# A hybrid mLSTM/RWKV-7 layer: PSUM banks, chain steps over two pairs, and the place of preparation and chain in the order

## Chip, cores and metric

The kernel runs on one core of a Trainium2 chip. The metric is the device time of one execution in microseconds. The median of three runs before the change is 3376.81 us (3371.88 to 3381.96).

## What is computed

One layer of a diffusion backbone over 512 latent tokens of width 2048, with 256 context tokens as a prefix, all in float32.

1. The condition vectors (one for the latents, one for the context) go through silu and the matrix w_mod and give shifts, scales and gates (the "modulation", 12288 columns).
2. The RMS-normalised and modulated tokens go through one input projection w_in. Half of the heads are mLSTM (4 heads), the others RWKV-7 (16 heads of 64, handled in 8 pairs of 128 channels), each in both directions. Context runs first; the latent scans start from the context's final states.
3. RWKV-7 per token: `S = S diag(w) - (S kk)(kk*a)^T + v k^T`, `y = S r`. Both directions are added, normalised per head, a bonus term is added, and the sum is multiplied with a gate.
4. Both halves are concatenated, go through w_out, and are added to x with a gate. A gated feed-forward part follows (up and gate projection, 3x3 depthwise convolution on the 8x64 grid, GELU, down projection), then a last RMS norm.

## The kernel before, in words

**Matmuls.** A weight tile is loaded (`wload`, L337), split into a high part and a rest (`whi` on ACT, `wlo` on DVE, L299 and L300), and each product is made of three matmuls (L370 to L372 for tiles of 128 channels by 512 tokens, L403 to L405 for token-major ones). The projection of one 128-column tile for the latents is 48 matmuls.

**RWKV in chunks of 64 tokens.** It has three stages per pair of heads. *Preparation* (`pair_shared`, `prep`, `bonus`): decays, keys and removal vectors are computed on ACT and DVE, then per half of the 512 columns two PSUM tiles take key-by-key products (L747), DVE masks them into `r_Gp` (L750), PE transposes the decayed keys (L759), ACT copies them into `r_sg` (L763), and everything goes to DRAM as the chunks' operands (`Sc_d` for the context, `Sx_d` for the latents). A context pair does both directions at once; a latent pair does one after the other. `bonus` (L931) ends a latent pair's preparation with the ACT copy of L941. The SBUF tiles of preparation (`r_kr`, `r_sg`, `r_KR`, `r_BK`, `r_Gp`, ...) have one buffer each. *Solve* (`tsolve`): the triangular systems of all chunks of two pairs are inverted, first 32x32 blocks by 30 steps on DVE (L798, L799), then two rounds of small matmuls (L816, L821). *Chain* (`chain`, `chain_step`): the state goes from chunk to chunk, 4 chunks for the context, 8 for the latents, both directions in one call: products with the state and with V, an ACT copy (`r_Rs`, L872), products, an ACT copy (`r_U`, L880), products, then DVE updates the states (L892) and adds the outputs (L899, L901). A call takes one pair, and has two PSUM banks; the two pairs of a job take turns, c by c.

**PSUM.** All eight banks are given to three tags (L126): `acc` for projections, `pre` for preparation, modulation sums, normalisation sums and the mLSTM heads, `R` for solve and chain (and L209).

**Order.** The program is traced in one order; a list scheduler then gives each instruction to its engine's queue by a simulated timeline: among those that could start, the one with the lowest number goes first. `tc.high_priority(n)` takes n off the numbers inside it. In the kernel before, only weight loads and splits have that, with 3000 (L343). Each engine runs its own queue strictly in the order that comes out. In the traced order, the loop over latent pairs (L1222) does: projections of the next pair, then `x_job(p)` (L1154): for even p from 2 a solve of two pairs, for odd p from 3 a chain of two pairs, then preparation of pair p; after it mLSTM gates (for p = 0) and a piece of the late modulation (`ada_late`, DVE sums over w_mod, L232). Behind the loop come the last solve, the last chain, the four mLSTM heads' projections (`x_head`), and the mLSTM heads themselves (`mlstm_head`; those marked early use preparation's SBUF tiles, the solve's `t_X` among them). The output projection is in two halves; the first (`out_first`, L1267) needs mLSTM heads 0 and 1 and RWKV pairs 0 to 3.

Of the kernel before, what the change touches and what calls it, by code (L numbers as in the profile page):

```python
# [11 lines left out]
ALU = mybir.AluOpType  # L12
# [3 lines left out]
P = 128  # L16
# [70 lines left out]
FIN_O = 1  # L87
EARLY_AT = (1, 2, 4, 4)
PRELOAD = True
TCOPT = dict(schedule_with_timeline_sim=True)  # L90


# [4 lines left out]
def body(tc, A, dbg=None):  # L97
# [25 lines left out]
    wp = Pool("wp")  # L123
    hp = Pool("hp")
    sm = Pool("sm")
    PB = {"acc": 2, "pre": 2, "R": 4}  # L126

    def PS(tag, shape):
        return ps.tile(list(shape), F32, tag=tag, name=nm(tag), bufs=PB[tag])
# [14 lines left out]
    rk = Pool("rk")  # L144
# [504 lines left out]
    LOHI = (slice(0, 64), slice(64, 128))  # L649
# [9 lines left out]
    def pair_shared(p, seg):  # L659
        n = NX if seg == "x" else NC_  # L660
        s = K()
        s.kr = rp("r_kr", [P, NX])
        s.kk = rp("r_kk", [P, NX])
        sp.dma_start(s.kr[:, :n], kr_d[seg][p])
        act.activation(s.kk[:, :n], s.kr[:, :n], AF.Copy, scale=V("rkk", p))
        sq = rp("r_t1", [P, NX])
        act.activation(sq[:, :n], s.kk[:, :n], AF.Square)
        pn = PS("pre", [P, 512])
        pe.matmul(pn[:, :n], bones, sq[:, :n], start=True, stop=True)
        act.activation(sq[:, :n], pn[:, :n], AF.Ln, bias=BK12)  # L670
        act.activation(sq[:, :n], sq[:, :n], AF.Exp, scale=-0.5)
        dve.tensor_tensor(s.kk[:, :n], s.kk[:, :n], sq[:, :n], ALU.mult)
        if seg == "x":
            s.r = rp("r_r", [P, NX])
            sp.dma_start(s.r, r_d[p])
        s.up = rp("r_up", [P, 2, 2, P])
        sp.dma_start(s.up, A["rup"][p])
        return s
# [159 lines left out]
            sp.dma_start(t[hs], v_d[seg][p // 2, :, :, o:o + 64].rearrange("a (b t) v -> t (a b) v", t=64))  # L838
        return t

    def chain_step(us, ops, cs, V, y, first, last):

        x = us[0].seg == "x"
        kc = us[0].kc
        bank = [PS("R", [P, 8, 64]) for _ in range(2)]
        pos = (0, 1) if cs[0] < cs[1] else (1, 0)
        opened = {}

        def mm(h, half, o, w, rhs):

            hs = LOHI[h]
            out = bank[h][LOHI[half], o, :]
            at = opened.get((h, half))
            f = dict(stop=True, skip_group_check=True)
            if at is None:
                opened[(h, half)] = pe.matmul(out, w[hs], rhs[hs], start=True, **f)
                return
            with tc.issue_after(at.ins):
                pe.matmul(out, w[hs], rhs[hs], start=False, **f)  # L859

        w = [o[:, c % 2] for o, c in zip(ops, cs)]
        kinds = range(2) if x else range(1)
        for src in range(2):
            for k, u in enumerate(us):
                for j in kinds:
                    for h in range(2):
                        o = 2 * kc * src + 64 * j
                        mm(h, h if j == 0 else 1 - h, pos[k], w[k][:, o:o + 64], u.M if src == 0 else V[:, cs[k], :])
        Rs = rk("r_Rs", [P, 2, 64], 3)
        U = rk("r_U", [P, 2, 64], 3)  # L870
        for h, hs in enumerate(LOHI):
            act.copy(Rs[hs], bank[h][hs, 0:2, :])  # L872
        for k, u in enumerate(us):
            for h in range(2):
                mm(h, 1 - h, 2 + pos[k], w[k][:, kc:kc + 64], Rs[:, pos[k], :])
            for h in range(2):
                if not last:
                    mm(h, h, 2 + pos[k], w[k][:, 3 * kc + 64:3 * kc + 128], V[:, cs[k], :])
        for h, hs in enumerate(LOHI):
            act.copy(U[hs], bank[h][LOHI[1 - h], 2:4, :])  # L880
        for k, u in enumerate(us):
            for h in range(2):
                if not last:
                    mm(h, h, 2 + pos[k], w[k][:, 3 * kc:3 * kc + 64], U[:, pos[k], :])
            for h in range(2):
                if x:
                    mm(h, 1 - h, pos[k], w[k][:, kc + 64:kc + 128], U[:, pos[k], :])
        if not last:
            for k, u in enumerate(us):
                g = u.g0 + cs[k]  # L890
                for h, hs in enumerate(LOHI):
                    dve.scalar_tensor_tensor(u.M[hs], u.M[hs], u.gC[hs, g:g + 1], bank[h][hs, 2 + pos[k], :], ALU.mult, ALU.add)  # L892
        if x:
            lo, hi = min(cs), max(cs)
            for h in range(2):
                hs = LOHI[1 - h]
                out = y[hs, lo:hi + 1:hi - lo, :]
                if first:
                    dve.tensor_copy(out, bank[h][hs, 0:2, :])  # L899
                else:  # L900
                    dve.tensor_tensor(out, bank[h][hs, 0:2, :], out, ALU.add)  # L901

    def chain(pairs, mid):

        x = pairs[0][0].seg == "x"
        nch = pairs[0][0].nch
        Vs, ys = [], []
        for us in pairs:
            Vs.append(chain_v(us[0].p, us[0].seg, nch))
            ys.append(rk("r_yt", [P, 8, 64], 2) if x else None)  # L910
            for u in us:
                if not x:
                    Mst[(u.p, u.d)] = rk("r_M", [P, 64], 16)
                    pool.memset(Mst[(u.p, u.d)], 0.0)
                u.M = Mst[(u.p, u.d)]
        n = nch // 2
        for i in range(n):
            if x and i == 1:
                mid()
            ops = [[chain_load(u, i if u.d == 0 else n - 1 - i) for u in us] for us in pairs]  # L920
            for c in range(2 * i, 2 * i + 2):
                for us, o, V, y in zip(pairs, ops, Vs, ys):
                    chain_step(us, o, (c, nch - 1 - c), V, y, c < nch // 2, x and c == nch - 1)
        if x:
            for us, y in zip(pairs, ys):
                y_d = us[0].y_d = DT("yr_d", [4, P, 128], 8)
                for h in range(2):
                    sp.dma_start(y_d[:, :, 64 * h:64 * h + 64].rearrange("a (b t) v -> t (a b) v", t=64), y[LOHI[1 - h]])
            mid()
# [215 lines left out]
    def ctx_job(p):  # L1145
        do_chain()
        job = []
        for pp in range(p, p + 2):
            s = pair_shared(pp, "c")
            job.append((pp, prep(pp, s, "c", DT("Sc_d", [P, 8, 320], 8)), None))  # L1150
        do_solve()
        solve_q.append(job)

    def x_job(p):  # L1154
        if p < 2:
            do_chain()
        elif p % 2 == 0:
            do_solve(2)
        else:
            do_chain(2)  # L1160
        s = pair_shared(p, "x")
        S_d = DT("Sx_d", [P, 16, 512], 8)
        us = prep(p, s, "x", S_d, 0) + prep(p, s, "x", S_d, 1)
        job = [(p, us, bonus(p, us[0], us[1], s))]
        if p == 0:
            do_solve()
        solve_q.append(job)
# [333 lines left out]
```

## Time and profile before

| | |
|---|---|
| median of 3 runs | 3376.81 us |
| profiled execution | 3379.97 us, span 3378.2 us |
| mean granted clock of TensorE | 0.945 |
| PE, PE weight loads, DVE, ACT busy | 3108.0, 2509.7, 2165.9, 1192.4 us |
| DMA | 548.53 MB, 162 GB/s on average |

The span runs from the first to the last instruction of the profiled execution; the execution's own time is 1.8 us longer. PE is TensorE's matmuls, PEld its weight loads, DVE, ACT and POOL the other engines, SP the queue that issues most DMAs. A granted clock of 1.0 is TensorE's full rate. "Releaser" is what ended a wait by the semaphores' records.

### The profile page before, as it was taken

The numbers are of one execution on the slowest core, as the hardware profiler recorded it, in microseconds if no ns is written. First come the engines' busy times: TensorE is split into PE (matmuls) and PEld (weight loads), VectorE is DVE, ScalarE is ACT, GpSimd is POOL, SyncE is SP. The second block draws the span as 40 slices with busy tenths as digits, with TensorE's granted clock in tenths as the row PEclk, the third lists the DMA queues.
The fourth block names the chain that finished last, engine by engine and source line by source line (L and its number), as shares of the span: only waits on it lengthen the run. The fifth ranks groups of instructions, "written<-read, shape, count | busy, mean of one in ns | idle before, by whom it ended". The sixth has DMA issues, their size and how long they took to land.

```text
span 3378.2 us, 54574 instructions
## 1 busy us (share of the span) xinstructions
PE 3108.0 (92%) x21030; PEld 2509.7 (74%) x21030; DVE 2165.9 (64%) x4178; ACT 1192.4 (35%) x2414; POOL 59.6 (2%) x113
## 2 busy tenths in 40 slices
PE   8998899999989898657599899999999999999998
PEld 5687777777768687545477688888888888888887
DVE  2587776688688778645644788455555555555657
ACT  4355554344444344222223432222222222322323
POOL 0000100010000000000000000000000000000000
PEclk9999998899989898767799999999999999999999
DMA  8877555557767687565844255222223222222232
GB/s 284 305 243 220 155 159 163 166 174 234 208 208 239 215 247 240 181 197 178 257 153 157 77 199 194 94 94 98 95 95 99 94 96 98 94 98 96 94 100 100
DMA packets 394387, 548.53 MB, mean 162 GB/s; under 512 B 151664, under 2 KB 272776, under 8 KB 393872
## 3 DMA queue, kind: packets, MB, share of 16 engines
q1 hardware_dynamic: 384480, 531.67, 49.3%
q10 hardware_dynamic: 9648, 13.37, 1.1%
q8 instruction: 166, 2.72, 0.3%
q14 instruction: 93, 0.76, 0.1%
HBM read 457.49 MB, written 87.47 MB: 161 GB/s over the span
## 4 chain that ended last, share of the span: by engine, by line
PE 53%; DMA 9%; DVE 6%; ACT 1%; issue 1%; SPq 1%; DVEq 0%; ACTq 0%
PE acc L371 10%; PE acc L372 10%; PE acc L370 10%; PE acc L1376 5%; PE acc L1378 5%; PE acc L1377 5%; DMA am<-in_wmod 3%; PE acc L1262 1%; PE pre L621 1%; PE acc L1263 1%; PE acc L1264 1%; DVE adacc L232 1%; DMA Sx_d<-r_sg 1%; PE R L859 1%; DMA x_d<-ev 1%
## 5 line engine op out<-in xcount | busy, mean ns | idle before, releaser
L299 ACT CAST whi<-wraw 128x512 fp32r<-128x512 f32 (+1 forms) x948 | 569.6, 604 | 1307.7 <-PE acc L371 678.6
L300 DVE TENSOR_TENSOR wlo<-wraw,whi 128x512 fp32r<-128x512 f32 (+1 forms) x948 | 628.4, 666 | 429.0 <-ACT whi L299 423.1
L370 PE MATMUL acc<-H,whi 128*128 128x512 f32 x1920 | 761.2, 396 | 6.1 <-ACT ev L520 4.0
L372 PE MATMUL acc<-H,wlo 128*128 128x512 f32 x1920 | 762.3, 397 | 1.2 <-DVE wlo L300 1.2
L371 PE MATMUL acc<-H,whi 128*128 128x512 f32 x1920 | 760.4, 396 | 0.0
L370 PEld LDWEIGHTS acc<-H,whi 128*128 128x128 f32 x1920 | 363.8, 189 | 87.5 <-ACT ev L520 4.3
L372 PEld LDWEIGHTS acc<-H,wlo 128*128 128x128 f32 x1920 | 364.2, 190 | 82.0 <-issue 4.9
L371 PEld LDWEIGHTS acc<-H,whi 128*128 128x128 f32 x1920 | 364.4, 190 | 78.8 <-issue 2.9
L1380 DVE SCALAR_TENSOR_TENSOR x<-acc,mod,x 128x512 f32<-128x512 f32 (+1 forms) x192 | 135.6, 706 | 221.7 <-PE acc L1378 221.6
L1324 DVE SCALAR_TENSOR_TENSOR f_cv<-upad,fvec,f_cv 128x512 f32<-128x512 f32 x352 | 263.8, 749 | 7.2
L1376 PE MATMUL acc<-fh,whi 128*128 128x512 f32 x640 | 253.2, 396 | 0.0
L1377 PE MATMUL acc<-fl,whi 128*128 128x512 f32 x640 | 253.1, 396 | 0.0
L1378 PE MATMUL acc<-fh,wlo 128*128 128x512 f32 x640 | 253.1, 396 | 0.0
L232 DVE SCALAR_TENSOR_TENSOR adacc<-am,csil,adacc 128x512 f32<-128x512 f32 x240 | 179.4, 748 | 83.7 <-DMA am<-in_wmod 81.6
L403 PE MATMUL acc<-whi,H 128*128 128x256 f32 x512 | 159.8, 313 | 2.2 <-ACT r_E L720 1.5
L405 PE MATMUL acc<-wlo,H 128*128 128x256 f32 x512 | 158.6, 311 | 1.6 <-DVE wlo L300 1.6
L404 PE MATMUL acc<-whi,H 128*128 128x256 f32 x512 | 156.0, 305 | 0.0
L1378 PEld LDWEIGHTS acc<-fh,wlo 128*128 128x128 f32 x640 | 120.2, 188 | 29.1
L1377 PEld LDWEIGHTS acc<-fl,whi 128*128 128x128 f32 x640 | 120.2, 188 | 29.0
L1376 PEld LDWEIGHTS acc<-fh,whi 128*128 128x128 f32 x640 | 120.2, 188 | 29.0
L1262 PE MATMUL acc<-H,whi 128*128 128x512 f32 x256 | 104.6, 414 | 32.4 <-DVE ev L1271 18.6
L750 DVE TENSOR_TENSOR r_Gp<-pre,c_gmask 64x512 f32<-64x512 f32 (+1 forms) x192 | 115.1, 599 | 18.1 <-DMA Sx_d<-r_Gp 11.6
(346 smaller groups left out, 4751.6 us busy)
## 6 DMA issues: line engine op xcount, KB each, us to landing
am<-in_wmod SPq DMA_DIRECT2D x128, 512.0 KB
wraw<-in_wup SPq DMA_DIRECT2D x88, 512.0 KB
wraw<-in_wgate SPq DMA_DIRECT2D x88, 512.0 KB
wraw<-in_wdn SPq DMA_DIRECT2D x88, 512.0 KB
wraw<-in_wcm SPq DMA_DIRECT2D x72, 512.0 KB
r_GK<-Sx_d SPq DMA_DIRECT2D x64, 512.0 KB
wraw<-in_wtm SPq DMA_DIRECT2D x56, 512.0 KB
Sx_d<-r_Gp SPq DMA_DIRECT2D x32, 512.0 KB
```

The lines of the kernel that those rows point to most:

```text
L232: dve.scalar_tensor_tensor(acc, wm[:, k % 2], csil[:, k:k + 1], acc, ALU.mult, ALU.add)
L299: act.copy(hi, t)
L300: dve.tensor_tensor(lo, t, hi.bitcast(F32), ALU.subtract)
L370: pe.matmul(pt[:, :n], hi(k8), H.h(k), start=k == 0, stop=False)
L371: pe.matmul(pt[:, :n], hi(k8), H.l(k), start=False, stop=False)
L372: pe.matmul(pt[:, :n], lo(k8), H.h(k), start=False, stop=k == KT - 1)
L403: pe.matmul(o, H.h(k)[:, xs], hi(k4), start=first, stop=False, skip_group_check=True)
L405: pe.matmul(o, H.h(k)[:, xs], lo(k4), start=False, stop=k == KT - 1, skip_group_check=True)
L1324: dve.scalar_tensor_tensor(cv, u[:, a:a + GH, b:b + GW], fvec[:, f, tap:tap + 1], cv, ALU.mult, ALU.add)
L1376: pe.matmul(pt, hi(m)[:, k, :], th[:, cs], start=k == 0, stop=False)
L1377: pe.matmul(pt, hi(m)[:, k, :], tl[:, cs], start=False, stop=False)
L1378: pe.matmul(pt, lo(m)[:, k, :], th[:, cs], start=False, stop=k == GF - 1)
```

## The change

`pre` gets four PSUM banks and `R` two. `chain_step` takes the units of all pairs of a job in one call (for a job of two pairs four units), with one pair of banks, one set of `r_Rs` and `r_U` tiles (one buffer each), and copies that are twice as wide; products with V come before those with the state. Chain steps, and the preparation of every pair (`pair_shared`, `prep`, `bonus`), are traced under `high_priority(1500)`. Chunk loads (`chain_load`) and solves are not.

```diff
--- before.py
+++ after.py
@@ -87,6 +87,7 @@
 FIN_O = 1
 EARLY_AT = (1, 2, 4, 4)
 PRELOAD = True
+AHEAD_C = 1500
 TCOPT = dict(schedule_with_timeline_sim=True)
 
 
@@ -123,7 +124,7 @@
     wp = Pool("wp")
     hp = Pool("hp")
     sm = Pool("sm")
-    PB = {"acc": 2, "pre": 2, "R": 4}
+    PB = {"acc": 2, "pre": 4, "R": 2}
 
     def PS(tag, shape):
         return ps.tile(list(shape), F32, tag=tag, name=nm(tag), bufs=PB[tag])
@@ -838,12 +839,12 @@
             sp.dma_start(t[hs], v_d[seg][p // 2, :, :, o:o + 64].rearrange("a (b t) v -> t (a b) v", t=64))
         return t
 
-    def chain_step(us, ops, cs, V, y, first, last):
-
-        x = us[0].seg == "x"
-        kc = us[0].kc
+    def chain_step(units, first, last):
+
+
+        x = units[0][0].seg == "x"
+        kc = units[0][0].kc
         bank = [PS("R", [P, 8, 64]) for _ in range(2)]
-        pos = (0, 1) if cs[0] < cs[1] else (1, 0)
         opened = {}
 
         def mm(h, half, o, w, rhs):
@@ -858,47 +859,48 @@
             with tc.issue_after(at.ins):
                 pe.matmul(out, w[hs], rhs[hs], start=False, **f)
 
-        w = [o[:, c % 2] for o, c in zip(ops, cs)]
-        kinds = range(2) if x else range(1)
-        for src in range(2):
-            for k, u in enumerate(us):
-                for j in kinds:
+        for src in (1, 0):
+            for u, w, c, V, n in units:
+                for j in range(2 if x else 1):
                     for h in range(2):
                         o = 2 * kc * src + 64 * j
-                        mm(h, h if j == 0 else 1 - h, pos[k], w[k][:, o:o + 64], u.M if src == 0 else V[:, cs[k], :])
-        Rs = rk("r_Rs", [P, 2, 64], 3)
-        U = rk("r_U", [P, 2, 64], 3)
+                        mm(h, h if j == 0 else 1 - h, n, w[:, o:o + 64], V[:, c, :] if src else u.M)
+        Rs = rk("r_Rs", [P, 4, 64], 1)
+        U = rk("r_U", [P, 4, 64], 1)
         for h, hs in enumerate(LOHI):
-            act.copy(Rs[hs], bank[h][hs, 0:2, :])
-        for k, u in enumerate(us):
+            act.copy(Rs[hs], bank[h][hs, 0:4, :])
+        for u, w, c, V, n in units:
             for h in range(2):
-                mm(h, 1 - h, 2 + pos[k], w[k][:, kc:kc + 64], Rs[:, pos[k], :])
+                mm(h, 1 - h, 4 + n, w[:, kc:kc + 64], Rs[:, n, :])
             for h in range(2):
                 if not last:
-                    mm(h, h, 2 + pos[k], w[k][:, 3 * kc + 64:3 * kc + 128], V[:, cs[k], :])
+                    mm(h, h, 4 + n, w[:, 3 * kc + 64:3 * kc + 128], V[:, c, :])
         for h, hs in enumerate(LOHI):
-            act.copy(U[hs], bank[h][LOHI[1 - h], 2:4, :])
-        for k, u in enumerate(us):
+            act.copy(U[hs], bank[h][LOHI[1 - h], 4:8, :])
+        for u, w, c, V, n in units:
             for h in range(2):
                 if not last:
-                    mm(h, h, 2 + pos[k], w[k][:, 3 * kc:3 * kc + 64], U[:, pos[k], :])
+                    mm(h, h, 4 + n, w[:, 3 * kc:3 * kc + 64], U[:, n, :])
             for h in range(2):
                 if x:
-                    mm(h, 1 - h, pos[k], w[k][:, kc + 64:kc + 128], U[:, pos[k], :])
+                    mm(h, 1 - h, n, w[:, kc + 64:kc + 128], U[:, n, :])
         if not last:
-            for k, u in enumerate(us):
-                g = u.g0 + cs[k]
+            for u, w, c, V, n in units:
+                g = u.g0 + c
                 for h, hs in enumerate(LOHI):
-                    dve.scalar_tensor_tensor(u.M[hs], u.M[hs], u.gC[hs, g:g + 1], bank[h][hs, 2 + pos[k], :], ALU.mult, ALU.add)
+                    dve.scalar_tensor_tensor(u.M[hs], u.M[hs], u.gC[hs, g:g + 1], bank[h][hs, 4 + n, :], ALU.mult, ALU.add)
         if x:
-            lo, hi = min(cs), max(cs)
-            for h in range(2):
-                hs = LOHI[1 - h]
-                out = y[hs, lo:hi + 1:hi - lo, :]
-                if first:
-                    dve.tensor_copy(out, bank[h][hs, 0:2, :])
-                else:
-                    dve.tensor_tensor(out, bank[h][hs, 0:2, :], out, ALU.add)
+            for k in range(0, len(units), 2):
+                cs = [units[k][2], units[k + 1][2]]
+                lo, hi = min(cs), max(cs)
+                y = units[k][0].y
+                for h in range(2):
+                    hs = LOHI[1 - h]
+                    out = y[hs, lo:hi + 1:hi - lo, :]
+                    if first:
+                        dve.tensor_copy(out, bank[h][hs, k:k + 2, :])
+                    else:
+                        dve.tensor_tensor(out, bank[h][hs, k:k + 2, :], out, ALU.add)
 
     def chain(pairs, mid):
 
@@ -919,8 +921,14 @@
                 mid()
             ops = [[chain_load(u, i if u.d == 0 else n - 1 - i) for u in us] for us in pairs]
             for c in range(2 * i, 2 * i + 2):
-                for us, o, V, y in zip(pairs, ops, Vs, ys):
-                    chain_step(us, o, (c, nch - 1 - c), V, y, c < nch // 2, x and c == nch - 1)
+                units = []
+                for k, (us, os_, V, y) in enumerate(zip(pairs, ops, Vs, ys)):
+                    us[0].y = y
+                    for j, (u, o) in enumerate(zip(us, os_)):
+                        cu = nch - 1 - c if j else c
+                        units.append((u, o[:, cu % 2], cu, V, 2 * k + (j if 2 * c < nch - 1 else 1 - j)))
+                with tc.high_priority(AHEAD_C):
+                    chain_step(units, c < nch // 2, x and c == nch - 1)
         if x:
             for us, y in zip(pairs, ys):
                 y_d = us[0].y_d = DT("yr_d", [4, P, 128], 8)
@@ -1146,8 +1154,9 @@
         do_chain()
         job = []
         for pp in range(p, p + 2):
-            s = pair_shared(pp, "c")
-            job.append((pp, prep(pp, s, "c", DT("Sc_d", [P, 8, 320], 8)), None))
+            with tc.high_priority(AHEAD_C):
+                s = pair_shared(pp, "c")
+                job.append((pp, prep(pp, s, "c", DT("Sc_d", [P, 8, 320], 8)), None))
         do_solve()
         solve_q.append(job)
 
@@ -1158,10 +1167,11 @@
             do_solve(2)
         else:
             do_chain(2)
-        s = pair_shared(p, "x")
-        S_d = DT("Sx_d", [P, 16, 512], 8)
-        us = prep(p, s, "x", S_d, 0) + prep(p, s, "x", S_d, 1)
-        job = [(p, us, bonus(p, us[0], us[1], s))]
+        with tc.high_priority(AHEAD_C):
+            s = pair_shared(p, "x")
+            S_d = DT("Sx_d", [P, 16, 512], 8)
+            us = prep(p, s, "x", S_d, 0) + prep(p, s, "x", S_d, 1)
+            job = [(p, us, bonus(p, us[0], us[1], s))]
         if p == 0:
             do_solve()
         solve_q.append(job)
```

## Rows read from the trace of the kernel before

**Rows 1.** The page: busy time and instructions; busy tenths and clock in 40 slices
```profile
PE 3108.0 (92%) x21030; PEld 2509.7 (74%) x21030; DVE 2165.9 (64%) x4178; ACT 1192.4 (35%) x2414; POOL 59.6 (2%) x113
PE   8998899999989898657599899999999999999998
PEclk9999998899989898767799999999999999999999
```

**Rows 2.** Windows: stretch, length, busy PE, PEld, DVE, ACT, POOL, clock, DMA share, GB/s
```profile
860.00:1366.00 506.00, 459.21 (x5677) 372.95 (x5676) 389.33 (x864) 216.51 (x499) 8.96 (x25) 0.91 0.72 226
1366.00:1476.00 110.00, 56.29 (x522) 43.13 (x520) 66.68 (x154) 22.96 (x48) 0.00 (x0) 0.66 0.61 179
1476.00:1676.00 200.00, 137.45 (x1283) 103.43 (x1284) 111.60 (x278) 63.10 (x189) 1.72 (x8) 0.75 0.68 220
1520.00:1540.00 20.00, 14.95 (x246) 12.78 (x238) 11.11 (x36) 7.60 (x27) 0.00 (x0) 0.50 0.89 297
```

**Rows 3.** Windows of L941 alone, cut at its copies; stretch, its length, ACT
```profile
661.00:787.00 126.00, 0.17 (x1) 0.97 0.61 190
787.00:886.00 99.00, 0.17 (x1) 0.97 0.69 202
886.00:961.00 75.00, 0.17 (x1) 0.93 0.72 224
961.00:1052.00 91.00, 0.17 (x1) 0.94 0.68 209
1052.00:1152.00 100.00, 0.17 (x1) 0.92 0.78 248
1152.00:1246.00 94.00, 0.17 (x1) 0.91 0.72 217
1246.00:1367.00 121.00, 0.17 (x1) 0.87 0.72 237
```

**Rows 4.** Single lines: count, least/median/longest ns, first and last start
```profile
L525 ACTq DMA_DIRECT2D r_d<-ev x8: 326/326/340, 466.5 to 860.5; - x8
L664 SPq DMA_DIRECT2D r_kr<-kr_x x8: 320/327/1541, 541.9 to 1222.3; - x8
L821 PE MATMUL R<-t_Y,t_X x768: 191/191/258, 424.0 to 1470.4; 32*32 32x32 f32 x192
L642 SPq DMA_DIRECT2D hm_d<-r_r x6: 319/320/326, 1534.4 to 1749.0; - x6
```

**Rows 5.** Waits of PE from 1400 to 1700 us: total, times, longest
```profile
PE pre L238 <- DVE adacc L232: 22.9, 1, 22.9
PE R L816 <- DVE t_X L810: 20.9, 2, 11.2
PE acc L1262 <- DVE ev L1271: 18.6, 1, 18.6
```

**Rows 6.** Waits of PE from 860 to 1400 us
```profile
PE R L859 <- ACT r_U L880: 7.9, 6, 1.7
PE pre L759 <- DVE r_cum L756: 6.7, 2, 6.3
PE pre L747 <- DVE r_Gp L750: 5.9, 9, 1.6
PE R L856 <- DVE r_yt L899: 4.2, 8, 0.9
PE R L859 <- ACT r_Rs L872: 3.8, 4, 1.5
```

**Rows 7.** Waits of the whole run
```profile
ACT r_sg L704 <- DMA Sx_d<-r_sg: 26.5, 9, 7.8
```

**Rows 8.** Single lines of the chain and the preparation
```profile
L872 ACT COPY r_Rs<-R x192: 242/261/263, 440.7 to 1583.2; 64x128 f32<-64x128 f32 x192
L763 ACT COPY r_sg<-pre x192: 352/367/372, 296.4 to 1365.9; 64x256 f32<-64x256 f32 x192
L892 DVE SCALAR_TENSOR_TENSOR r_M<-r_M,r_gC,R x352: 252/278/294, 449.9 to 1581.3; 64x64 f32<-64x64 f32 x176
```

## The prediction

> **What bounds the kernel now.** I read the page first, then the windows, then single lines. The page [rows 1] shows TensorE busy for 92% of the span, and in its slice line the exceptions: slices 16 to 19 fall to 5 to 7 tenths, and the granted clock with them. So most of the kernel is matmul work, and the only large hole is near the middle. The windows [rows 2] give its size: from 860 to 1366 us PE is busy 459.21 of 506 us (91%); from 1366 to 1476 it is 56.29 of 110, from 1476 to 1676 it is 137.45 of 200, both at a clock of 0.66 to 0.75; behind that the page's slices are dense again. The hole holds 116 us of idle PE, and what runs there runs largely at the lower of the clock's two levels (1.2 GHz of 2.4).
>
> What ends late there? The RWKV part is a pipeline: preparation of a pair, solve of two pairs, chain of two pairs. The last instruction of each pair's preparation is the ACT copy of L941; cutting the trace at those copies [rows 3] gives the time between one pair and the next: 126, 99, 75, 91, 100, 94 and 121 us, 706 us for seven pairs. It is serial, since its SBUF tiles have one buffer each. Its inputs do not hold it: the last of the projected tiles that it reads leaves for DRAM at 860.5, and the last pair's keys are read back at 1222.3 [rows 4]. From 860 on the projections that are left (the mLSTM heads') are pure filler, and they have run out when pair 7's preparation ends at 1366. Then solve(6,7) (its last matmul at 1470.4), the heads 0 and 1, which need its tiles (their first hm written at 1534.4), and the dense output projection at 1676 follow one another with little beside them: PE's longest waits there are on the modulation sums, on the solve's transposes and on the output projection's own start [rows 5]. So the preparation is the path, and its end pulls some 310 us of latency behind it, bare.
>
> **The change, part by part.** *Preparation gets four PSUM banks and a place 1500 instructions earlier.* With two banks, the second half's matmuls (L747) wait until DVE has emptied the first half's banks, then the transposes (L759) wait again. PE's own waits on that in 860 to 1400 are 5.9 and 6.7 us [rows 6], small, because a filler matmul stands in between; the pair's latency is what counts. The place matters more: solves, gates, finalizing, modulation sums and keeps hold their place and fall behind preparation and chain, and the mLSTM heads' weight splits, which stand 3000 ahead, keep less of their lead. The 126 us interval has the mLSTM gates in it, which stand between pair 0 and pair 1; the 121 us one has pieces of finalizing and the chain. Bounds: nothing gained (0), or every pair as quick as the best, 75 us: 706 - 7 x 75 = 181 us. I take as attainable the mean of the three shortest intervals, (75 + 91 + 94)/3 = 87 us, and cap the longer ones by it: 39 + 12 + 0 + 4 + 13 + 7 + 34 = 109 us, nearer to the upper rows than to zero since one pair already reached 75 with two banks.
>
> What stays in that interval: r_sg and r_Gp have one buffer each, and a tile is free again only when its write to DRAM has landed; at L704 alone ACT's waits on that are 26.5 us over the whole run, 7.8 us the longest [rows 7]. The change leaves them.
>
> *What is late next.* The 310 us behind preparation (solve, heads, start of the output projection) move up as a piece. Is there engine time? PE's work between 860 and 1676 is 459 us plus, in the hole, 194 us at a mean clock of about 0.72, at the upper level some 139: 598 us. In 816 - 109 = 707 us that is a share of 85%, below the 91% it had from 860 to 1366. DVE has 389 + 67 + 112 = 568 us [rows 2], a share of 80%, where it had 77%: just room. If DVE cannot pass 77%, 568/0.77 = 738 us and the gain is 78. If only PE's 91% binds, 598/0.91 = 657 us and it is 159; that is the low end.
>
> *Chain steps take both pairs in one pair of banks.* There were 96 calls with 192 ACT copies of 64x128 at L872 and as many at L880, 261 ns each [rows 8], 100 us; now 48 steps with 192 copies of 64x256, which take 367 ns on the nearest row, L763 [rows 8], 70 us. ACT gets 30 us back, which buys nothing: it is busy 43% of 860 to 1366. State updates (278 ns [rows 8]) and output adds stay as many, and so do the matmuls. The V products now stand before those of the state; they gain nothing, because the bank they open is free only when the previous step's outputs have been read. What is lost: two calls had banks of their own, so one pair's matmuls ran while the other pair's copies and updates did. PE's waits inside chain lines in 860 to 1400 are 7.9 + 4.2 + 3.8 us [rows 6], about 16. Bounds: no change, or 48 bare steps (rival 3). I take 10 us, the nearer row, as most gaps have a filler matmul behind them.
>
> *Two banks fewer for solves.* The second pair's products now need the first's banks; in the trace they come after the reload of the one-buffer t_Y and its transpose, which is what PE waits for [rows 5]. Cost 0; if that cover goes, another wait of that size, 20.9 us in the hole, is the bound, and a solve that gets done sooner is the other. The modulation columns of L209 have the tag too, but are made before the first chain.
>
> *Queue order.* Moved preparation issues its DMAs (rup, kr, r, KR, G, BK) on SP earlier as well, past weight loads. SP's weight loads have three buffers and 3000 instructions of lead; I take 0, since the DMA share in that stretch is 0.72 [rows 2]; were a weight load late once per pair by the longest wait of rows 7, it would be 8 x 7.8 = 62 us, inside the range's upper part; were tiles freed sooner, a few us of gain. Chunk loads for the chain keep their place, though the steps that use them move; a step then waits for its load, as it did.
>
> Sum: -109 + 10 = -99 us on the profiled run's 3380.0 us: 3281. That run lies 3 us above the median, so **3278 us**.
>
> A rule of the Trainium skill speaks against the change: "PSUM — Partial Sum Buffer", section "Engine vs sequencer instructions", says that matmuls start and complete in program order. A chain matmul put in front of ready projection matmuls then holds them all until its copy arrives. The trace agrees as far as it goes, since chain waits do show on PE, but at 16 us. By the rule alone the sum would be rival 3's.
>
> **The rivals.**
> 1. *The interval is set by one-buffer tiles and DVE, not by banks or place.* For: DVE is busy 77% there, and r_sg waits for its writes to land [rows 7]. Against: the 75 us pair had the same buffers. Then only the interval with the gates in it shortens, 39 us, less 10 for the chain: 3348 us.
> 2. *The places do not change.* The instruction order comes from a simulated timeline which takes the first ready instruction; a preparation that waits for its own tiles is no earlier for a better number. For: pairs follow each other closely. Against: gates and finalizing lie inside two intervals. Time: 3377, give or take 10.
> 3. *Slower: one pair of banks makes each step's latency bare.* Place: the chain lines on PE, in all 48 steps. Price of a bare step, by rows 8: four copies x 367 ns, eight state updates x 278, four output operations that I price as state updates: 1.5 + 2.2 + 1.1 = 4.8 us; 48 steps, 230 us. It decides from 109/48 = 2.3 us bare per step on. For: in 1520 to 1540, where chain steps stand nearly alone, the clock is 0.50 with PE "busy" 14.95 of 20 us [rows 2], so bare steps also run slow. Against: from 860 to 1366 the filler is there. With two thirds bare: +153 - 109 = +44, so 3421 us.
>
> **How the numbers follow.** Forecast 0.55, rival 1 0.20, rival 2 0.09, rival 3 0.16. Within 0.3% (10 us, about what this kernel's measurement can tell from no change) falls most of rival 2; forecast and rival 1 are faster: faster 0.75, same 0.08, slower 0.17. The range: PE's bound of 159 us plus a few us from context pairs gives 3210 below; above, it takes in rivals 1 and 2 and the first part of rival 3, to 3395. The forecast's own range is 3225 to 3310.
>
> **What would show it.** Right: L941's last copy near 1260 instead of 1366, intervals at or under 90 us, the gates behind pair 1's preparation, heads' projections still on PE when the last chain runs, the slices 16 to 19 at 8 or 9 tenths with the clock near 1.0, dense output projection from about 1575. Wrong: L941 ends past 1330 (rival 1 or 2), or PE's idle time at L856 and L859 grows from some 16 us to over 100 (rival 3), or the solve, which was not moved, stretches: its recurrence (L798, L799) stands behind boosted DVE work.

## The result, and the profile after

The changed kernel takes 3410.19 us (median of three, 3409.91 to 3413.8) against 3376.81: a ratio of 1.0107, interval 1.0082 to 1.0131. It is slower by 33 us where 3278 us, 99 us faster, had been forecast. The profiled execution took 3409.91 us, its span 3408.1 us.

The page of the kernel after: busy time and instructions, then busy tenths and TensorE's clock in 40 slices.

```profile
PE 3078.4 (90%) x21030; PEld 2503.2 (73%) x21030; DVE 2172.0 (64%) x4178; ACT 1179.4 (35%) x2235; POOL 51.9 (2%) x113
PE   8998888989999975667498899999999999999998
PEclk9999889999999996567699999999999999999999
```

Against [rows 1], PE does the same 21030 matmuls with 30 us less busy time in a span that is 30 us longer, so it is idle for 60 us more. The slices at 7 tenths or less, 16 to 19 before, are now 14 to 19: the hole begins two slices earlier and ends in the same one.

Windows of the kernel after: the stretches of [rows 2], same columns.

```profile
860.00:1366.00 506.00, 435.37 (x5092) 359.78 (x5090) 322.91 (x734) 170.39 (x330) 4.07 (x11) 0.92 0.64 193
1366.00:1476.00 110.00, 62.45 (x988) 55.61 (x988) 70.71 (x197) 25.09 (x60) 0.51 (x3) 0.51 0.59 172
1476.00:1676.00 200.00, 145.17 (x1496) 110.15 (x1496) 115.33 (x287) 66.86 (x166) 1.78 (x8) 0.76 0.71 230
```

From 860 to 1366, DVE is busy 322.91 us where it was 389.33. The forecast had feared that DVE would have too much to do; it had too little. Part of that work had moved to before 860, as the next view shows; the rest stood still.

Windows of the preparation's last line (L949, L941 before), cut at its copies as in [rows 3]: stretch, length, ACT busy, clock, DMA share, GB/s.

```profile
577.00:673.00 96.00, 0.17 (x1) 0.98 0.58 184
673.00:731.00 58.00, 0.17 (x1) 0.97 0.82 255
731.00:791.50 60.50, 0.17 (x1) 1.00 0.61 196
791.50:852.00 60.50, 0.17 (x1) 0.97 0.90 268
852.00:1188.00 336.00, 0.17 (x1) 0.98 0.62 187
1188.00:1258.00 70.00, 0.17 (x1) 0.95 0.67 216
1258.00:1400.00 142.00, 0.17 (x1) 0.66 0.69 199
```

This is the reading that matters. Pair 1 takes 96 us, and three pairs follow at 58 to 61 us, well below the 87 us that the forecast took as attainable. Pair 4 ends at 851, where it ended at 1051 before: 200 us gained, 84 of them already at pair 0 (576 against 660). Then pair 5 takes 336 us, and pair 7, the last, 142 us. Preparation ends at 1399 instead of 1366, 33 us later, which is also what the kernel lost.

What held pair 5? Three views of the kernel after. First all instructions on tiles of tag `pre` in three stretches (windows: PE, PEld, DVE, ACT busy, clock, DMA share, GB/s); second ACT's timeline at 839; third PE's timeline at 1122 (start, duration, line, tiles).

```profile
791.00:852.00 61.00, 13.97 (x104) 8.96 (x104) 8.91 (x14) 7.97 (x19) 0.97 0.89 266
852.00:1122.60 270.60, 1.05 (x8) 1.09 (x9) 2.92 (x5) 1.46 (x4) 0.99 0.60 178
1122.60:1188.00 65.40, 14.85 (x110) 10.00 (x110) 11.76 (x17) 9.45 (x22) 0.97 0.72 226
```

```profile
838.97 0.63 ACT L668 ACTIVATE r_t<-r_kk 128x512 f32<-128x512 f32 x1
```

```profile
1122.47 0.39 PE L371 MATMUL acc<-H,whi 128*128 128x512 f32 x1
1122.70 0.27 PE L979 MATMUL pre<-c_ident,r_y 128*128 128x128 f32 x1
1122.81 1.02 PE L670 MATMUL pre<-r_t,c_bones 128*128 128x512 f32 x2
```

Pair 5's squared keys (`r_t`, L668) are ready at 839.6. The matmul that reads them, L670, starts at 1122.81. From 852 to 1122.6, 270 us, the four banks of `pre` see eight matmuls of 1.05 us in all, done by 855.5: after that they lie empty. L670 starts right behind L979, the first of finalize's transposes for pair 0, which takes a tile of the same tag. The order of the built program's instructions says the same. Two pairs of neighbours on PE, by line, output and inputs:

```
L979 MATMUL pre_1963_11511<-c_ident_7_90,r_y_1918_10975 128x128
L670 MATMUL pre_1974_11550<-r_t1_1973_11548,c_bones_8_92 128x512
L979 MATMUL pre_2198_13127<-c_ident_7_90,r_y_2153_12591 128x128
L670 MATMUL pre_2209_13166<-r_t1_2208_13164,c_bones_8_92 128x512
```

Tiles are numbered as they are traced. Finalize's tile (1963) was traced before pair 5's (1974), and pair 7's (2209) behind another of finalize's (2198); in both places the boosted matmul stands directly behind the unboosted one. A tag's buffers are handed out in traced order, free or not, so a lead of 1500 does not carry an instruction past an earlier user of its tag. Finalize of pair 0 needs chain(0,1), and so preparation of pair 5 did too.

The same happens in tag `R`. Single lines of the kernel after from 890 to 1200 (solve's recurrence for pairs 2 and 3; the copies of chain(0,1); the two rounds of solve's products for pairs 2 and 3): least/median/longest ns, first and last start.

```profile
L800 DVE TENSOR_TENSOR t_X<-t_X,t_T x30: 178/349/408, 962.6 to 993.1; 128x30 f32<-128x30 f32 x2, 128x58 f32<-128x58 f32 x2, 128x84 f32<-128x84 f32 x2, 128x108 f32<-128x108 f32 x2
L871 ACT COPY r_Rs<-R x16: 365/367/368, 966.8 to 1092.9; 64x256 f32<-64x256 f32 x16
L817 PE MATMUL R<-t_X,t_Y x128: 191/191/212, 1102.5 to 1126.8; 32*32 32x32 f32 x128
L822 PE MATMUL R<-t_Y,t_X x128: 191/191/212, 1107.0 to 1133.2; 32*32 32x32 f32 x128
```

The recurrence ends at 993, the products begin at 1102.5, when the chain in the same two banks has ended. The last solve is late too: L822 lasts to 1490.4 (1470.4 in [rows 4]); the first hm write comes at 1543.0 (1534.4) and the last at 1773.5 (1749.0).

```profile
L822 PE MATMUL R<-t_Y,t_X x768: 191/191/257, 400.5 to 1490.4; 32*32 32x32 f32 x192
L643 SPq DMA_DIRECT2D hm_d<-r_r x6: 319/320/423, 1543.0 to 1773.5; - x6
```

So the delay is not handed on one for one: 33 us at preparation's end, 20 at the solve's, 9 at the first hm write, 24.5 at the last, 30 at the end of the profiled execution.

PE's waits of the kernel after: 860 to 1400 us (answers to [rows 6]), then 1400 to 1700 ([rows 5]); total, times, longest.

```profile
PE R L860 <- ACT r_Rs L871: 13.1, 4, 5.4
PE R L860 <- DMA r_GK<-Sx_d: 13.1, 6, 4.9
PE R L817 <- DVE t_X L811: 11.2, 1, 11.2
PE pre L760 <- DVE r_cum L757: 10.2, 5, 6.3
```

```profile
PE pre L979 <- DVE r_y L973: 28.4, 2, 18.8
PE R L857 <- issue: 16.0, 4, 6.3
PE R L860 <- DMA r_GK<-Sx_d: 12.6, 7, 4.0
```

No row names the 270 us. PE is fed with projections meanwhile, so nothing idles that a list of waits could show; only the dates of one line give it away. The bill comes when the projections run out, and there the longest wait is again on finalize's transposes. But the waits on the chain's own lines (L857, L860) come to more in sum: 39 us from 860 to 1400 and 61 from 1400 to 1700, where the kernel before has 20.5 (the prediction's 16 are its three largest rows) and 14 on its L856 and L859.

### The profile page after: what moved, and what is told of

It is laid out like the page before. It is cut to its first block, busy times and chain, and to the rows that moved or that the text cites. A ratio compares the mean times of both kernels' runs of the same rounds, so it can differ in the third digit from the quotient of the medians.

```text
span 3408.1 us, 54206 instructions
## 1 busy us (share of the span) xinstructions
PE 3078.4 (90%) x21030; PEld 2503.2 (73%) x21030; DVE 2172.0 (64%) x4178; ACT 1179.4 (35%) x2235; POOL 51.9 (2%) x113
## 4 chain that ended last, share of the span: by engine, by line
PE 67%; DMA 13%; DVE 12%; ACT 3%; issue 3%; SPq 1%; POOL 0%; DVEq 0%; ACTq 0%
PE acc L373 11%; PE acc L371 11%; PE acc L372 11%; PE acc L1386 4%; PE acc L1388 4%; PE acc L1387 4%; DMA am<-in_wmod 4%; DVE adacc L233 2%; PE pre L196 2%; PE acc L1272 2%; PE R L860 2%; PE acc L1273 2%; PE acc L1274 1%; DVE r_Gp L751 1%; DVE wlo L301 1%
## 5 line engine op out<-in xcount | busy, mean ns | idle before, releaser
L406 PE MATMUL acc<-wlo,H 128*128 128x256 f32 x512 | 150.8, 296 | 2.6 <-DVE wlo L301 2.6
L405 PE MATMUL acc<-whi,H 128*128 128x256 f32 x512 | 151.0, 295 | 0.0
L404 PE MATMUL acc<-whi,H 128*128 128x256 f32 x512 | 149.2, 292 | 0.0
```

The lines of the kernel that those rows point to most:

```text
L405: pe.matmul(o, H.l(k)[:, xs], hi(k4), start=False, stop=False, skip_group_check=True)
```

## The experiments

Ratios are to the kernel before, from runs on the same chip, three rounds each. Two theories went in: that tags handed out in traced order undo the lead (A), and that the merged chain step is a loss by itself (B); with a third, that the lead starves the solve (C).

**1. The lead alone** (`pri_only`): the old banks and calls, chain steps and preparation under the lead.

```diff
-                    chain_step(us, o, (c, nch - 1 - c), V, y, c < nch // 2, x and c == nch - 1)
+                    with tc.high_priority(AHEAD_C):
+                        chain_step(us, o, (c, nch - 1 - c), V, y, c < nch // 2, x and c == nch - 1)
```

(The same `with` around the preparation of context and latent pairs, as in the change, is left out here.)

> The kernel before with only the places moved: chain steps and preparation 1500 instructions ahead; PSUM banks and chain steps as before. Theory A (the loss comes from the banks: a tag's buffers are handed out in the traced order, so preparation waits for finalizing, and with two R banks the solve waits for the whole chain ahead of it): 3355 to 3385 us, within 0.6% of before. Rival B (a chain step over four units is itself too long): also near before, 3355 to 3385. Rival C (moved preparation and chain starve the solve, which was not moved): slower, 3395 us or more.

Measured 3367.62 us, 1.0002 (0.9986 to 1.0017); preparation ends at 1362, with 152 us for pair 5. By itself the lead changes nothing in the time.

**2. Banks and merged steps without the lead** (`banks_only`).

```diff
-AHEAD_C = 1500
+AHEAD_C = 0
```

> The changed kernel with the lead of 1500 set to 0: only the banks (4, 2) and the merged chain step are left of the change. Theory A and rival B: still slow, 3395 to 3420 us. Rival C: the loss is gone, 3377 us or less.

Measured 3393.17 us, 1.0077 (1.005 to 1.0105). That is 2 us under the range of A and B; C falls. Pair 4 ends at 895, pair 5 at 1170: the stop is there without any lead.

**3. Finalize in a bank of its own** (`fin_bank`).

```diff
-    PB = {"acc": 2, "pre": 4, "R": 2}
+    PB = {"acc": 2, "pre": 3, "R": 2, "fin": 1}
-        pt = PS("pre", [P, 512])
+        pt = PS("fin", [P, 512])
```

> The changed kernel, with the transposes of finalizing in a bank of their own (pre 3, fin 1, R 2). Theory A: preparation of pair 5 starts right behind that of pair 4 instead of 270 us later, the last preparation ends near 1100 instead of 1399 us; if that was the whole of the loss, 3300 to 3350 us. Rival B, and the part of A about the two R banks: preparation gets early all the same, but solve and chain still alternate at about 185 us per two pairs, and the time stays at 3390 to 3420 us. Rival C: no change, 3400 to 3420.

Measured 3370.45 us, 1.0005 (0.9989 to 1.0021): the loss is gone, and so is the stop at pair 5, which takes 76 us. Preparation's last operand is written at 1177 (1395 in the kernel after). The time lies between the two ranges, 20 us from either: the stop was the loss against the kernel before, but without it the time does not fall below that kernel's, so something else bounds it there.

**4. The solve in the lead too** (`solve_pri`).

```diff
-            tsolve([us for job in jobs for _, us, _ in job])
+            with tc.high_priority(AHEAD_C):
+                tsolve([us for job in jobs for _, us, _ in job])
```

> The changed kernel with the solve moved 1500 ahead as well. Rival C: 3330 to 3375 us. Theory A and rival B: the recurrence on DVE gets shorter by some 20 us per job, but its products still wait for the chain's banks: 3395 to 3415 us.

Measured 3399.74 us, 1.0104 (1.0068 to 1.014): C falls. The solve's place in the order is not what delays it.

**5. Merged steps and lead, banks as before** (`merge_only`).

```diff
-    PB = {"acc": 2, "pre": 4, "R": 2}
+    PB = {"acc": 2, "pre": 2, "R": 4}
```

> The changed kernel with the banks of before (pre 2, R 4): merged chain steps and the lead of 1500 stay. Theory A (the two R banks and the wait of preparation for finalizing make the loss): with four R banks chain and solve no longer alternate strictly, but preparation still waits for finalizing; 3360 to 3385 us. Rival B (a merged step is itself longer: its one chain of products, copies and updates passes behind projection matmuls three times, with no second pair under way): chains stay at 120 us or more per job and the time at 3390 to 3415 us.

Measured 3387.18 us, 1.0052 (1.0035 to 1.0068). That lies between the two ranges. At these banks the merged calls add 17 us (1.0052 against 1.0002 in experiment 1); with the banks of the change they do the opposite, as the next run shows, so the loss does not divide into a part for each.

**6. Lead and new banks, calls not merged** (`split_r2`): experiment 1 with the other banks.

```diff
-    PB = {"acc": 2, "pre": 2, "R": 4}
+    PB = {"acc": 2, "pre": 4, "R": 2}
```

> The complement: the banks of the change (pre 4, R 2) and the lead of 1500, but chain calls of one pair as before, so that the two pairs' calls take turns on one pair of banks. Theory A: the two R banks are the cost, and the merged step was only their repair; a chain job takes over 150 us and the time is over 3430 us. Rival B: two short calls pass no slower than one long one; 3380 to 3410 us.

Measured 3503.95 us, 1.0405 (1.0389 to 1.042). A holds. With two banks in `R` the merged call is far better than single ones. Pair 5 takes 441 us here, behind finalize and a chain(0,1) of 173 us (126 in the kernel after).

**7. Solve and finalize apart from everything** (`solve_bank`): the kernel after, with a fourth tag.

```diff
-    PB = {"acc": 2, "pre": 4, "R": 2}
+    PB = {"acc": 2, "pre": 2, "R": 2, "S": 2}
-            ws = [PS("R", [P, 16, 32])[:, 0:nc_] for _ in range(2)]
+            ws = [PS("S", [P, 16, 32])[:, 0:nc_] for _ in range(2)]
-        pt = PS("pre", [P, 512])
+        pt = PS("S", [P, 512])
```

> The changed kernel with acc 2, pre 2, R 2 and two banks S for the solve's products and for finalizing: neither the solve waits for the chain's banks nor preparation for finalizing. Theory A: both waits are gone, chain jobs follow one another without the 45 us of solve between them; 3320 to 3360 us. Rival B: the merged steps still take 16 to 20 us each beside projections, four jobs of 130 us or more in a row; 3375 us or more.

Measured 3329.9 us, **0.9892** (0.9875 to 0.9908), faster than both kernels; A holds. Its recurrence for pairs 2 and 3, its products and the copies of chain(0,1):

```profile
L800 DVE TENSOR_TENSOR t_X<-t_X,t_T x30: 192/350/409, 941.1 to 1022.0; 128x30 f32<-128x30 f32 x2, 128x58 f32<-128x58 f32 x2, 128x84 f32<-128x84 f32 x2, 128x108 f32<-128x108 f32 x2
L817 PE MATMUL S<-t_X,t_Y x128: 191/191/255, 1034.2 to 1076.0; 32*32 32x32 f32 x128
L822 PE MATMUL S<-t_Y,t_X x128: 191/191/212, 1046.5 to 1082.5; 32*32 32x32 f32 x128
L871 ACT COPY r_Rs<-R x16: 350/367/368, 922.3 to 1064.8; 64x256 f32<-64x256 f32 x16
```

The products start 12 us after the recurrence, while the chain still runs; in the kernel after it was 109 us. Preparation ends at 1327 with no interval above 102 us behind the first.

**8. The lead, and finalize in tag `R`** (`pri_finR`): experiment 1 with one more edit.

```diff
-        pt = PS("pre", [P, 512])
+        pt = PS("R", [P, 512])
```

> The kernel before with the lead of 1500, and finalizing's transposes in the chain's tag R: preparation never waits for finalizing. If preparation is what bounds the kernel before (the prediction's reading), its last copy moves from 1362 us in the kernel with the lead alone to 1250 to 1300 us, and the time falls to 3300 to 3340 us. If solve and chain bound it as much, preparation gets early and the time stays within 15 us of 3368.

Measured 3342.0 us, 0.9922 (0.9907 to 0.9937). Preparation ends at 1296, as expected if it bounds the kernel; the time is 2 us above the range for that. With finalize out of preparation's tag the lead is worth 26 us; with it in, nothing (experiment 1).

**9. The same with merged steps** (`merge_finR`): experiment 5 with the edit of 8.

> Merged chain steps and the lead, banks as before (acc 2, pre 2, R 4), finalize's transposes in tag R instead of pre. Against its twin without merged steps (0.992 of before) this shows what merging costs once preparation no longer waits for finalize. Theory A (banks are handed out in traced order, and what is lost is lost through that): preparation ends near 1300 as in the twin, the merged steps' extra length (12 to 25 us per job of two pairs) stands beside filler, so 0.990 to 0.995, 3335 to 3352 us. Theory B (the merged step is a loss by itself): the 17 us that merging cost with banks as before come again, 0.997 or more, 3357 us or more.

Measured 3346.68 us, 0.9938 (0.9912 to 0.9964), which overlaps with 8: a cost of the merged step by itself does not show. A holds, B falls; preparation ends at 1320. From first to last `r_Rs` copy, the four latent chains together take 477 us here and 543 us in 8: under the lead, merged ones are shorter. In the kernel before, with neither, they take 456, and in the kernel after 530.

**10. Finalize in `R` alone** (`before_finR`): the kernel before with the edit of 8.

> The kernel before with one edit: finalize's transposes in tag R instead of pre; no lead, no merged step. Theory A: the wait of pair 7 on finalize goes, some 20 to 50 us of preparation, with or without the lead: 0.990 to 0.995, 3335 to 3352 us, last preparation copy near 1300 to 1330. Rival (the lead is what moves preparation, and only the tag stood in its way): without the lead preparation stays behind finalize and solve in the order: 0.998 to 1.002, 3360 to 3375 us, last copy near 1360.

Measured 3371.31 us, 1.0011 (0.9994 to 1.0027); preparation ends at 1359. The rival was right: the tie costs nothing as long as preparation is not early. With these banks and calls, the lead and finalize's untied tag gain only together.

**11. Experiment 7 without the lead** (`sb_lead0`), the edit of 2.

> The version with two banks each for acc, pre, R and S (solve's products and finalize in S; 0.989 of before), its lead set from 1500 to 0. Theory A: with the tags apart, the order of readiness does the work and the lead adds little: 0.987 to 0.992, 3324 to 3340 us. Theory C (the lead, not the tags, decides): preparation and chain steps fall back behind finalize and solves, 0.997 or more, 3357 us or more.

Measured 3346.29 us, 0.9932 (0.991 to 0.9954), outside both expectations: untied tags bring two thirds of the gain of 7, the lead the last third. Preparation ends at 1373, 7 us later than in the kernel before, and still the kernel is faster; its end alone does not set the time.

**12. Experiment 7 with single calls** (`sb_split`): the tags of 7 in the kernel of 1.

> The same tags and lead (acc, pre, R and S two banks each), with chain steps of one pair per call as before. Theory A: an unmerged step holds both R banks, so the two pairs take turns with nothing beside them, as with R 2 and four pre banks (1.0405): 1.01 to 1.03, 3400 to 3470 us; last chain of two pairs takes over 160 us. Theory B (the merged step is the loss): the unmerged one is quicker, 0.984 or less, under 3315 us.

Measured 3332.14 us, 0.9903 (0.9874 to 0.9933): both theories missed. The last chain takes 201 us, as A expected, and all four together 762, but the time is that of 7. So a long chain costs little where nothing else waits for its banks. The 1.0405 of experiment 6 came with the two ties that this run cuts together, finalize with preparation and solve with chain; how it divides between them was not tried.

**13 and 14. One tie each, from the kernel after.** `after_finR` has the edit of 8; in `after_S` only the solve moves:

```diff
-    PB = {"acc": 2, "pre": 4, "R": 2}
+    PB = {"acc": 2, "pre": 2, "R": 2, "S": 2}
-            ws = [PS("R", [P, 16, 32])[:, 0:nc_] for _ in range(2)]
+            ws = [PS("S", [P, 16, 32])[:, 0:nc_] for _ in range(2)]
```

> The kernel after with one edit: finalize's transposes in tag R, where solve and chain already share two banks; preparation keeps its four to itself. Theory A (traced order within a tag; preparation was held by finalize, and chain and solve hold each other in R): preparation no longer stops behind pair 4, its last copy comes before 1240 us (after: 1399), but the gain is lost again in R, where chain, solve and finalize now all wait for each other in traced order: 0.998 to 1.006, the first latent chain ends past 1150 us as with finalize in a bank of its own. Rival (preparation's stop is the whole loss): with it gone the time falls to what the lead and an untied finalize gave with four R banks, 0.990 to 0.994.

> The kernel after with solve's products in two banks of their own, taken from preparation (acc, pre, R and S two each); finalize stays in pre. Theory A: chain and solve no longer hold each other, so chain(0,1) ends earlier than the 1093 us of after; preparation still waits for finalize, but finalize comes sooner with the chain: 0.997 to 1.003, last preparation copy 1350 to 1375. Rival (finalize in preparation's tag is the whole loss): as bad as the version with merged steps and banks as before, 1.005 or more.

`after_finR` measured 3373.96 us, 1.0011 (0.9999 to 1.0024); `after_S` 3406.1 us, 1.0116 (1.0082 to 1.015), where A had expected at most 1.003 and the rival 1.005 or more: the rival was right. Single lines of `after_finR`: preparation's operand writes and its last line; then, from 990 to 1400, the recurrence for pairs 2 and 3, chain(0,1), and two solves' products.

```profile
L765 SPq DMA_DIRECT2D Sx_d<-r_sg x32: 359/380/2225, 543.0 to 1082.6; - x32
L949 ACT COPY r_bo<-pre x8: 166/166/166, 577.6 to 1370.4; 128x8 f32<-128x8 f32 x8
L800 DVE TENSOR_TENSOR t_X<-t_X,t_T x30: 191/344/408, 996.6 to 1087.5; 128x30 f32<-128x30 f32 x2, 128x58 f32<-128x58 f32 x2, 128x84 f32<-128x84 f32 x2, 128x108 f32<-128x108 f32 x2
L871 ACT COPY r_Rs<-R x16: 351/368/370, 1007.8 to 1159.4; 64x256 f32<-64x256 f32 x16
L822 PE MATMUL R<-t_Y,t_X x256: 191/191/257, 1185.2 to 1377.8; 32*32 32x32 f32 x128
```

All operands that preparation makes are written by 1082.6, 284 us earlier than in the kernel before, and the time is that of before, as A had expected. Its last copy, L949, which dates preparation elsewhere, was expected before 1240 and comes at 1370.4: the bonus tile `r_bo` has six buffers, and the copies for pairs 6 and 7 start just after finalize's last read (L972) of the tiles of pairs 0 and 1, a further tie in traced order (in experiment 3 too: 1236 against 1177). The solve does not need that copy. What is left is that the solve waits: its recurrence ends at 1087.5, its products begin at 1178.8 (L817; their second round is shown), when chain(0,1) has left the banks, and those for pairs 4 and 5 end at 1377.8. In `after_S` it is the other way round; PE's timeline there at 1130:

```profile
1130.75 0.33 PE L979 MATMUL pre<-c_ident,r_y 128*128 128x128 f32 x1 [0.28 <-DVE r_y L973]
1130.91 1.02 PE L670 MATMUL pre<-r_t,c_bones 128*128 128x512 f32 x2
```

Pair 5 still waits for finalize, with 154 us, and preparation ends at 1402. So the four cases from the kernel after read: both ties 1.0107, finalize untied 1.0011, solve untied 1.0116, both untied 0.9892. (The versions with a fourth tag also have two `pre` banks instead of four.) Untying finalize takes back the 33 us; untying the solve is worth something only then, since until then preparation is later than the solve.

## Why the prediction was wrong

**The step that failed: "a place 1500 instructions earlier", with "solves, gates, finalizing, modulation sums and keeps hold their place and fall behind preparation and chain".** Finalizing did not fall behind: it takes a tile of `pre`, and a tag's tiles are handed out in traced order. Term by term: the forecast capped the six intervals above 87 us and gained 109. Up to pair 4 the gain was larger than that, 200 us: 84 before pair 0 was done, which the forecast did not count, and 116 in four intervals, where four banks and the lead gave 58 to 61 us behind the first; with the lead and two banks, in experiments 8 and 9, they were 77 to 103. Then pair 5's interval took 236 us more than before, pair 6's 24 less and pair 7's 21 more: 33 us lost in all. The forecast summed intervals as if each had its own cause; the path had another branch (chain, finalize, the next pair's first `pre` tile) that did not shorten with them. The clue stood in my own working: an interval with "pieces of finalizing and the chain" in it. I took the pieces for work that could be moved past, and did not ask whose banks they use.

**"Two banks fewer for solves ... Cost 0": wrong, but hidden.** I looked at what PE waited for in the old solve. What counted was who else asks for the two banks: recurrence to products 109 us in the kernel after, 12 us with banks of their own. It did not set the time while finalize did (1.0107 against 1.0116 with the solve untied); once finalize is out of the way it costs the difference between 1.0011 and 0.9892, about 40 us.

**"I take 10 us" for the merged step: not told apart from zero.** Single lines of the kernel after, as in [rows 8], and its wait that answers to [rows 7]:

```profile
L871 ACT COPY r_Rs<-R x96: 347/367/369, 441.4 to 1652.9; 64x256 f32<-64x256 f32 x96
L891 DVE SCALAR_TENSOR_TENSOR r_M<-r_M,r_gC,R x352: 262/280/306, 451.4 to 1646.3; 64x64 f32<-64x64 f32 x176
```

```profile
ACT r_sg L705 <- DMA Sx_d<-r_sg: 27.7, 11, 5.1
```

The copies take 367 ns as priced, the state updates stay, and so does the wait on preparation's writes (26.5 us before). By itself the step costs 5 us by the medians' ratios (9 against 8), but the two intervals overlap, so neither nothing nor 10 us is ruled out. With finalize tied to preparation it came to 17 us (5 against 1); that the stop behind finalize passes it on fits, since preparation ends at 1384 there and at 1362 in 1, but no run separates it.

**Rival 3 came nearest in time (3421); its cause holds only in part.** Its sign was over 100 us of PE's waits on the chain lines. From 860 to 1400 they are 39 us (the two rows of 13.1 and six small ones); with 1400 to 1700 they are 99.5, against 35 in the kernel before, so it is nearly met. But bare steps do not come with the merged step and its two banks by themselves: `solve_bank` has both, with 54 us of such waits from 860 to 1700, and is the fastest, and single calls with the same tags (experiment 12) take as long. In the kernel after the last chain runs from 1514 to 1653, behind the late solve and with the projections gone, where it ran from 1469 to 1583 before. That the ties made it late and bare fits; no run puts a price on it alone. The Trainium skill's page "PSUM — Partial Sum Buffer", section "Engine vs sequencer instructions", says that matmuls start and complete in program order; the timelines agree (L670 starts 0.11 us behind L979 above). What decided here was a wait between two users of one PSUM tag.

**What was read rightly, and by luck.** Preparation's end came 33 us later and the time rose by 33 us, but that the two are equal is luck: the delay shrank to 9 us at the first hm write and grew again to 24.5 at the last. In experiment 11 preparation ends 7 us later than in the kernel before and the time is 0.9932. That all behind it moves as a piece was therefore too simple. What the time does follow is the last hm write: in all sixteen profiled executions the end comes 1630 to 1643 us behind it.

**Open.** How the 40 us between `after_finR` and `solve_bank` divide is mostly told by experiment 3: there finalize has a bank of its own and the solve stays with the chain, at 1.0005, so taking finalize out of `R` gave next to nothing, and the gain came with the solve's own banks (with three and two banks for `pre`, which differ as well). A lead of another size was not tried.

## What to carry to other kernels

Before you move work up by priority, list what else takes buffers of the same tags, in traced order: here an early step waited for the earlier-traced user of its tag, even with banks lying empty, and inherited all that this user waited for. Give tags by who may wait for whom, not by how many banks a stage can fill: two banks each in four tags took 0.9892 where four and two took 1.0107, with the same steps. And when one branch is shortened, date the branches that meet it: here the lead and finalize's untied tag were each worth nothing alone, and 26 us together.

## What the runs showed of the chip

In 1366 to 1476 PE is busy for 62.45 of 110 us in the kernel after and for 56.29 in the kernel before ([rows 2]), yet the granted clock is 0.51 against 0.66: in the kernel after it stood almost wholly at the lower of its two levels (1.2 of 2.4 GHz). More busy time is not more work: busy time multiplied by the clock, an estimate from these rows, is about 32 us at the full rate in the kernel after and 37 before, and part of the longer busy time is the slower clock itself. That stretch holds chain(4,5) with little beside it, 988 matmuls where 522 stood before, the shorter ones (63 against 108 ns in the mean). I had taken the hole's clock as given by how empty it is; here the stretch with the larger busy share had the lower clock.
